# Column updates of a bisection on VectorE: one instruction on all columns, or one per column with a scalar operand

## The chip, the cores and the metric

The kernel runs on one core of a Trainium2 chip. Its engines are TensorE (PE in the profile, its weight loads PEld), VectorE (DVE), ScalarE (ACT), GpSimd (POOL) and SyncE (SP), which issues the DMAs here. Each engine takes its instructions in program order and waits for semaphores where an operand comes from elsewhere, or from an earlier instruction of its own that is still under way. The metric is the time of one execution on the device in microseconds (us), the median of the runs.

## What is computed

One decoder layer for 1024 tokens of width 1024, in float32. The part that matters here picks, for each query token, the 256 keys with the highest indexer score; softmax attention then runs over those keys alone:

```python
logits = jnp.einsum('bqhd,bsd->bqhs', iqb, ik_f) * (IDX_DIM ** -0.5)
score = jnp.einsum('bqh,bqhs->bqs', w, jax.nn.relu(logits))
score = jnp.where(causal[None], score, -jnp.inf)
_, idx = lax.top_k(score, k_sel)            # k_sel = 256
s = jnp.einsum('bqhd,bqkhd->bhqk', qb, kg) * (HEAD_DIM ** -0.5)
p = jax.nn.softmax(jnp.where(valid, s, -jnp.inf))
```

Around it stand one combined projection (q, k, v, indexer, pooling channels), a causal multi-scale pooling of 512 channels, an output projection, two layer norms with conditioning, and a gated feed-forward network.

## The kernel before, in words

The tokens lie in eight tiles of 128 rows; tile i has 128(i + 1) possible keys. Tiles 0 and 1 need no selection. For each of the others the kernel finds the 256th highest score of every row by bisection on the bits of the score, without sorting: `bisect` (line 643) first turns the scores into 16-bit keys, searches the upper half in 15 rounds, then the lower half in 16. A round counts for each row how many keys reach a candidate threshold (the buffer `cand`), and moves the candidate by half the last step, up or down.

Two engines search at once. ScalarE takes tiles 5 and 4 together and tile 3 (`search_a`, buffers colsA). VectorE takes tile 2 alone (buffers colsE, "the E search") and tiles 7 and 6 together (buffers colsD, "the D search"), in `search_v` (line 675). Such a buffer holds a few numbers per row of a tile; a number for each of nt tiles is nt neighbouring columns. A round of `search_v` has one counting pass per tile (lines 681 and 682: a tensor_scalar over up to 1024 keys whose accumulator gives the count; in the profile TENSOR_SCALAR_CACHE_REDUCE and DVE_READ_ACCUMULATOR) and then two small instructions on all nt columns at once: line 683 writes `pr`, the step where the count is high enough and zero otherwise, and line 685 adds it, with a constant, to `cand`. The next round's passes need that `cand`.

The search runs beside other work: the last indexer scores, the projections q, u, k and v on TensorE, the pooling and the rotary embedding on GpSimd. Places in VectorE's queue that others wait for are `u_split` (line 863: a pass over the pooling channels, written to ub_V, which ScalarE rounds to phi_V and GpSimd splits to plo_V for TensorE's matmuls "po"), and the two subtractions in `k_transpose` (kr_K, after TensorE's transposes kT and ScalarE's copies). GpSimd also splits the weights (ws_W) that TensorE multiplies with next. The attention (`u_exp`) begins with tile 7 and needs its finished selection.

The order on VectorE, ScalarE and GpSimd is fixed while the kernel is built. Every search is a Python generator that yields an engine and an estimated time before each piece. A `Queue` for each engine adds up its estimated time (`cost`, line 138; at least 0.16 us for any VectorE instruction), and `fill` (line 768) puts a search piece in wherever it is estimated to end before the next ordinary instruction could begin, give or take a slack. So more instructions in a round also move where later rounds stand. TensorE, and in the attention the other engines as well, are ordered by a scheduler.

Almost all instructions are issued by one helper line (169), so the profile's rows are told apart by the names of their buffers.

Of the kernel before, what the change touches and what calls it, by code (L numbers as in the profile page):

```python
# [18 lines left out]
ALU = mybir.AluOpType  # L19
# [162 lines left out]
def decoder_layer_kernel(  # L182
# [8 lines left out]
    V, A, G, T, SP = (Queue(tc, e, n, pinned, times) for e, n in  # L191
                      ((nc.vector, "V"), (nc.scalar, "A"), (nc.gpsimd, "G"), (nc.tensor, "T"), (nc.sync, "S")))
# [450 lines left out]
    def bisect(tiles, cols, on_act):  # L643

        nt = len(tiles)
        col = lambda q: cols[:, q * 4 : q * 4 + nt]
        cntc, kp, sg, cand, pr, M, ng, th, ib, thr = (col(q) for q in range(10))
# [3 lines left out]
        def trash(i):  # L651
            return ((junkA if 5 in tiles else junkB) if on_act else junkd(i))[:, 0 : P * (i + 1)]

        one = lambda c, m: c[:, m : m + 1]
# [20 lines left out]
        def search_v(bits, base, low):  # L675
            V.memset(cand, float(1 << (bits - 1)))
            for b in range(bits - 1, -1, -1):
                yield "V", 0.4 + 1.08 * sum_w + 0.35 * nt
                for m, i in enumerate(tiles):
                    dt = U16 if low else I16  # L680
                    V.tensor_scalar(trash(i).bitcast(dt), kv[i].bitcast(dt), one(cand, m), one(base, m),
                                    ALU.is_ge, ALU.add, accum_out=one(cntc, m))
                V.tensor_scalar(pr, cntc, 0.0, float(1 << b), ALU.is_ge, ALU.mult)
                off = -float(1 << (b - 1)) if b > 0 else -1.0
                V.scalar_tensor_tensor(cand, pr, off, cand, ALU.add, ALU.add)

        def search_a(bits, low):

# [13 lines left out]
            V.tensor_scalar(cand, cand, -1.0, None, ALU.mult)  # L702

        yield from (search_a(15, False) if on_act else search_v(15, kp, False))
        V.tensor_copy(M, cand)
        for m, i in enumerate(tiles):
# [5 lines left out]
            if on_act:  # L712
                V.tensor_scalar(one(thr, m), one(ng, m), 2.0, float(P * (i + 1) + 1), ALU.mult, ALU.add)
        yield from (search_a(16, True) if on_act else search_v(16, ng, True))

        V.tensor_copy(ib.bitcast(I32), M)
# [421 lines left out]
    for n_, u in enumerate(units):  # L1138
        g, pr, i = u
# [767 lines left out]
```

## Time and profile before

| what | value |
|---|---|
| time, median of 3 runs | 1324.58 us (1322.65 to 1326.92) |
| profiled execution: span | 1321.4 us |
| median of the runs less that span | 3.2 us |
| TensorE busy | 1199.6 us (91%) |
| VectorE busy | 1066.3 us (81%), 1828 instructions |
| GpSimd busy | 736.7 us (56%) |
| ScalarE busy | 648.6 us (49%) |

For the profiled execution the profile gives the span, from its first to its last instruction, and no other time of its own.

The page cuts the span into 40 slices of 33 us; a digit is the busy share in tenths:

```profile
PE   8979895797988996999789999999999999999996
...
DVE  6899999999978797477697787776878777777698
ACT  3346673675998776445534243333333333333531
POOL 1392373666213355427678384664848475576848
```

The searches on VectorE lie in slices 4 to 12 (about 117 to 374 us). VectorE is at 9 or more in nearly all of them, and TensorE dips to 5 and 7 in slices 7 and 8. The attention follows, to about 570 us, and then the output projection and the feed-forward part, where TensorE is busy almost throughout.

The rows of a timeline read: start in us, duration in us, engine, line, operation, output<-input, shapes and count; a bracket at the end gives how long the engine was idle before the row, and the instruction that ended the wait. A row with a count above one merges several.

### The profile page before, as it was taken

Reading aid. Unit: us, or ns where it says so; the run is one execution under the profiler, and the core shown is the slowest. Engines: PE = TensorE matmul, PEld = TensorE weight load, DVE = VectorE, ACT = ScalarE, POOL = GpSimd, SP = SyncE. Lnnn points to the kernel's source line nnn. Section 1 sums busy time; section 2 is a strip of 40 time slices with the busy share of each in tenths; the row PEclk is TensorE's granted clock in tenths of the full one; section 3 lists DMA queues with packets and bytes.
Section 4 is the critical chain, followed back from the end, with each engine's and each line's share of the span. In section 5 each row is a group of like instructions: output and inputs, shape, how many; then the busy total and the mean of one; then the engine's idle time right before and its main releaser. Section 6 shows DMA issues by size and latency. Waiting matters only on the chain.

```text
span 1321.4 us, 16106 instructions
## 1 busy us (share of the span) xinstructions
PE 1199.6 (91%) x5462; PEld 934.3 (71%) x5462; DVE 1066.3 (81%) x1828; ACT 648.6 (49%) x1335; POOL 736.7 (56%) x509
## 2 busy tenths in 40 slices
PE   8979895797988996999789999999999999999996
PEld 6646564575855654787677787878788887878775
DVE  6899999999978797477697787776878777777698
ACT  3346673675998776445534243333333333333531
POOL 1392373666213355427678384664848475576848
PEclk8999898798979998999799999999999999999998
DMA  9540020131100266420020101102010111113112
GB/s 343 222 158 29 16 72 24 64 96 42 47 16 9 73 215 239 144 72 9 32 96 32 65 32 64 64 32 96 33 64 32 65 43 53 68 44 112 47 58 119
DMA packets 34904, 103.91 MB, mean 79 GB/s; under 512 B 3843, under 2 KB 3843, under 8 KB 33286
## 3 DMA queue, kind: packets, MB, share of 16 engines
q1 hardware_dynamic: 34822, 102.88, 22.1%
q8 instruction: 43, 0.70, 0.2%
q14 instruction: 39, 0.32, 0.1%
HBM read 93.42 MB, written 9.45 MB: 78 GB/s over the span
## 4 chain that ended last, share of the span: by engine, by line
PE 38%; DVE 6%; POOL 4%; issue 2%; ACT 1%; DVEq 0%; POOLq 0%; ACTq 0%
PE gu L169 24%; PE dn L169 14%; DVE act_W L169 2%; POOL wraw_R L169 1%; DVE utmp_X L169 1%; POOL wraw_W L169 1%; DVE gtmp_V L169 1%; POOL wblk_T L169 0%; DVE wblk_T L169 0%; DVE hr_H L169 0%; POOL hr_H L169 0%; DVE res_X L169 0%; DVE stat_C L169 0%; POOL wblk_V L169 0%; DVE wblk_V L169 0%
## 5 line engine op out<-in xcount | busy, mean ns | idle before, releaser
L169 PE MATMUL gu<-hr_H,wblk_T 128*128 128x512 f32 (+1 forms) x924 | 217.3, 387 | 3.0 <-POOL wblk_T L169 1.9
L169 PE MATMUL gu<-hr_H,wblk_V 128*128 128x512 f32 (+1 forms) x924 | 215.2, 384 | 3.7 <-POOL wblk_V L169 1.9
L169 PEld LDWEIGHTS gu<-hr_H,wblk_T 128*128 128x128 f32 x924 | 172.3, 191 | 39.2 <-POOL wblk_T L169 3.6
L169 PEld LDWEIGHTS gu<-hr_H,wblk_V 128*128 128x128 f32 x924 | 170.0, 188 | 40.1 <-POOL wblk_V L169 3.6
L169 DVE TENSOR_TENSOR res_X<-res_X,dn 128x512 f32<-128x512 f32 (+1 forms) x253 | 159.0, 678 | 15.4 <-PE dn L169 15.3
L169 POOL TENSOR_SCALAR sm_H<-sm_H,stat_X 128x1024 f32<-128x1024 f32 (+7 forms) x64 | 58.6, 928 | 124.1 <-DVE stat_X L169 112.5
L169 PE MATMUL pj<-ws_W,hT_H 128*128 128x512 f32 x456 | 119.4, 409 | 4.4 <-ACT pout_K L169 2.0
L169 POOL TENSOR_TENSOR wraw_R<-wraw_R 128x512 f32<-128x512 f32 x64 | 94.5, 1484 | 46.9 <-DVE wblk_T L169 23.7
L169 POOL TENSOR_TENSOR wraw_W<-wraw_W 128x512 f32<-128x512 f32 x60 | 86.7, 1452 | 58.0 <-DVE wblk_V L169 29.3
L169 PEld LDWEIGHTS pj<-ws_W,hT_H 128*128 128x128 f32 x456 | 85.1, 192 | 30.0 <-issue 10.1
L169 PE MATMUL dn<-wblk_T,act_W 128*128 128x512 f32 x324 | 79.6, 394 | 4.4 <-DVE act_W L169 4.4
L169 PE MATMUL dn<-wblk_V,act_W 128*128 128x512 f32 x324 | 78.5, 391 | 2.9 <-DVE act_W L169 2.5
L169 DVE TENSOR_SCALAR_CACHE_REDUCE junk_X<-keysD_T,colsD_X 128x1024 int16<-128x1024 int16 (+1 forms) x64 | 78.9, 1269 | 0.7
L169 ACT ACTIVATE wblk_V<-wraw_R 128x512 fp32r<-128x512 f32 x56 | 35.2, 629 | 80.7 <-POOL wraw_R L169 62.3
L169 PEld LDWEIGHTS dn<-wblk_T,act_W 128*128 128x128 f32 x324 | 60.9, 189 | 19.1 <-DVE act_W L169 6.5
L169 PEld LDWEIGHTS dn<-wblk_V,act_W 128*128 128x128 f32 x324 | 60.4, 188 | 17.4 <-DVE act_W L169 4.2
L169 POOL TENSOR_TENSOR ws_W<-raw_R,ws_W 128x1024 fp32r<-128x1024 f32 x17 | 44.8, 2652 | 48.6 <-ACT ws_W L169 48.5
L169 ACT ACTIVATE wblk_V<-wraw_W 128x512 fp32r<-128x512 f32 x53 | 33.1, 627 | 75.0 <-POOL wraw_W L169 56.4
L169 ACT ACTIVATE wblk_T<-wraw_W 128x512 fp32r<-128x512 f32 x56 | 35.0, 628 | 66.3 <-POOL wraw_W L169 50.2
L169 ACT ACTIVATE wblk_T<-wraw_R 128x512 fp32r<-128x512 f32 x52 | 32.5, 627 | 60.9 <-POOL wraw_R L169 45.5
L169 ACT ACTIVATE junkA_T<-keys_T,colsA_X 128x768 bf16<-128x768 uint16 (+3 forms) x62 | 54.1, 873 | 9.0 <-DVE colsA_X L169 8.7
L169 ACT ACTIVATE utmp_X<-gu 128x512 f32<-128x512 f32 x33 | 19.7, 598 | 73.4 <-PE gu L169 73.4
(300 smaller groups left out, 2828.1 us busy)
## 6 DMA issues: line engine op xcount, KB each, us to landing
wm_K<-in_wma_dram SPq DMA_DIRECT2D x16, 512.0 KB, 9.5
modraw_V<-in_wmc_dram SPq DMA_DIRECT2D x16, 512.0 KB, 4.5
wraw_R<-in_wg_dram SPq DMA_DIRECT2D x6, 1024.0 KB, 4.9
wraw_R<-in_wd_dram SPq DMA_DIRECT2D x12, 512.0 KB, 3.5
wraw_W<-in_wup_dram SPq DMA_DIRECT2D x12, 512.0 KB, 3.5
modraw_V<-in_wmg_dram SPq DMA_DIRECT2D x10, 512.0 KB, 4.3
wraw_R<-in_wup_dram SPq DMA_DIRECT2D x10, 512.0 KB, 3.5
wraw_W<-in_wg_dram SPq DMA_DIRECT2D x5, 1024.0 KB, 4.9
```

Of the source, the lines that this page charges most:

```text
L169: ins_ = f(*a, **k)
```

## The change

```diff
@@ -680,9 +680,11 @@
                     V.tensor_scalar(trash(i).bitcast(dt), kv[i].bitcast(dt), one(cand, m), one(base, m),
                                     ALU.is_ge, ALU.add, accum_out=one(cntc, m))
-                V.tensor_scalar(pr, cntc, 0.0, float(1 << b), ALU.is_ge, ALU.mult)
                 off = -float(1 << (b - 1)) if b > 0 else -1.0
-                V.scalar_tensor_tensor(cand, pr, off, cand, ALU.add, ALU.add)
+                for m in range(nt):
+                    V.tensor_scalar(one(pr, m), one(cntc, m), 0.0, float(1 << b), ALU.is_ge, ALU.mult)
+                for m in range(nt):
+                    V.tensor_scalar(one(cand, m), one(pr, m), one(cand, m), off, ALU.add, ALU.add)
```

`one(c, m)` is column m of c. The update of `cand` was a scalar_tensor_tensor with two tensor inputs, `pr` and `cand`; now it is a tensor_scalar whose input is one column of `pr`, whose first scalar operand is the old candidate column and whose second is the constant. The value computed is the same. In the D search (nt = 2) a round now has four small instructions instead of two, in the E search (nt = 1) two as before; there are 31 rounds in each. The estimate that the generator yields for a round is as it was, but the `Queue` counts each instruction as it is issued, so a D round comes to 0.32 us more in it.

The places of the searches' pieces move with that. In the rows below, junk<-keysD is a counting pass of the D search, junk<-keysA with colsE one of the E search, and the rows on colsD or colsE alone are the small instructions. VectorE, the last rounds ahead of the second u_split, before:

```order
L169 TENSOR_SCALAR junk_X_614,colsE_X_616<-keysA_X_605,colsE_X_616 128x384
L169 TENSOR_SCALAR junk_X_607,colsD_X_615<-keysD_T_609,colsD_X_615 128x1024
L169 TENSOR_SCALAR junk_X_608,colsD_X_615<-keysD_T_609,colsD_X_615 128x896
L169 TENSOR_SCALAR colsE_X_616<-colsE_X_616 128x1
L169 TENSOR_SCALAR colsD_X_615<-colsD_X_615 128x2
L169 SCALAR_TENSOR_TENSOR colsE_X_616<-colsE_X_616 128x1
L169 SCALAR_TENSOR_TENSOR colsD_X_615<-colsD_X_615 128x2
L169 CAST colsE_X_616<-colsE_X_616 128x1
```

The same place now, from the last D round on:

```order
L169 TENSOR_SCALAR junk_X_607,colsD_X_615<-keysD_T_609,colsD_X_615 128x1024
L169 TENSOR_SCALAR junk_X_608,colsD_X_615<-keysD_T_609,colsD_X_615 128x896
L169 TENSOR_SCALAR colsD_X_615<-colsD_X_615 128x1
L169 TENSOR_SCALAR junk_X_614,colsE_X_616<-keysA_X_605,colsE_X_616 128x384
L169 TENSOR_SCALAR colsD_X_615<-colsD_X_615 128x1 x3
L169 TENSOR_SCALAR colsE_X_616<-colsE_X_616 128x1 x2
L169 TENSOR_SCALAR junk_X_614,colsE_X_616<-keysA_X_605,colsE_X_616 128x384
L169 TENSOR_SCALAR colsE_X_616<-colsE_X_616 128x1 x2
```

Behind these, four more E rounds of the last two rows follow before the CAST that ends the E search. Before, E's passes stood inside D's rounds there; now five of them stand alone. Ahead of the first u_split 26 E passes are issued instead of 30, and 12 D passes as before.

The second place is VectorE between the D search and the subtractions kr_K, at the end of the upper half of ScalarE's search. Before, these rows stood behind 42 D passes, and another D round came before the row on keys_T:

```order
L169 TENSOR_SCALAR colsA_X_606<-colsA_X_606 128x1
L169 TENSOR_TENSOR kr_K_1238<-kT_1902,kr_K_1238 64x4x128 x2
L169 TENSOR_SCALAR junk_X_607,colsD_X_615<-keysD_T_609,colsD_X_615 128x1024
L169 TENSOR_SCALAR junk_X_608,colsD_X_615<-keysD_T_609,colsD_X_615 128x896
L169 TENSOR_SCALAR colsD_X_615<-colsD_X_615 128x2
L169 SCALAR_TENSOR_TENSOR colsD_X_615<-colsD_X_615 128x2
L169 TENSOR_SCALAR junkA_T_612,colsA_X_606<-keys_T_611,colsA_X_606 128x768
```

Now, behind 40 D passes:

```order
L169 TENSOR_SCALAR junkA_T_612,colsA_X_606<-keys_T_611,colsA_X_606 128x768
L169 CAST colsA_X_606<-colsA_X_606 128x2
L169 SCALAR_TENSOR_TENSOR keys_T_611<-keys_T_611,colsA_X_606,score_X_77 128x768
L169 TENSOR_SCALAR colsA_X_606<-colsA_X_606 128x1
L169 TENSOR_SCALAR colsA_X_606<-colsA_X_606 128x2
```

The first kr_K now stands behind the row on keys_T, and every later kr_K has one D round fewer ahead of it, so one more stands behind the last: four instead of three. GpSimd's and SyncE's order is unchanged up to buffer numbers.

## The prediction

> **What bounds the kernel now.** I read the table of windows first, for the stretch in which the search runs. Its columns are the window, its length, then the busy time (and instructions) of TensorE, its weight loads, VectorE, ScalarE and GpSimd, the granted TensorE clock, the DMA share and GB/s.
>
> ```profile
> span 1321.4 us, 16106 instructions
> ...
> 244.00:283.00 39.00, 29.98 (x117) 23.02 (x116) 38.27 (x49) 27.75 (x68) 25.09 (x14) 0.87 0.31 95
> 283.00:330.00 47.00, 35.62 (x145) 28.25 (x144) 45.49 (x82) 26.83 (x61) 33.36 (x22) 0.89 0.16 51
> 330.00:372.00 42.00, 42.00 (x191) 34.04 (x190) 39.09 (x76) 40.41 (x121) 6.96 (x6) 1.00 0.11 38
> ```
>
> From 244 to 330 us VectorE is busy 83.8 of 86 us and TensorE 65.6: VectorE sets the pace. From 330 to 372 TensorE is busy throughout, at full clock, and ScalarE 40.4 of 42. So time taken from VectorE counts fully only until TensorE becomes the later one. Next come the groups of the search's small instructions (count, busy us, mean ns), and the minimum/median/maximum of the same from the view by tile. colsD is the search of tiles 7 and 6 ("D"), colsE that of tile 2 ("E").
>
> ```profile
> L169 DVE SCALAR_TENSOR_TENSOR colsD_X<-colsD_X 128x2 f32<-128x2 f32 x31 | 18.4, 592 | 0.7
> L169 DVE TENSOR_SCALAR colsD_X<-colsD_X 128x2 f32<-128x2 f32 x33 | 18.0, 546 | 0.8
> L169 DVE SCALAR_TENSOR_TENSOR colsE_X<-colsE_X 128x1 f32<-128x1 f32 x31 | 11.5, 371 | 0.6
> ...
> L169 DVE TENSOR_SCALAR colsD_X<-colsD_X x39: 130/170/2162, 181.0 to 367.4; 128x2 f32<-128x2 f32 x33, 128x1 f32<-128x1 f32 x4, 128x2 int16<-128x2 f32 x1, 128x2 int32<-128x2 int32 x1
> L169 DVE SCALAR_TENSOR_TENSOR colsD_X<-colsD_X x31: 156/161/2282, 194.9 to 360.3; 128x2 f32<-128x2 f32 x31
> L169 DVE TENSOR_SCALAR colsE_X<-colsE_X x37: 136/148/154, 117.9 to 241.6; 128x1 f32<-128x1 f32 x35, 128x1 int16<-128x1 f32 x1, 128x1 int32<-128x1 int32 x1
> L169 DVE SCALAR_TENSOR_TENSOR colsE_X<-colsE_X x31: 145/160/1265, 125.7 to 239.9; 128x1 f32<-128x1 f32 x31
> ```
>
> An instruction on two numbers per partition takes 0.16 us at the median and up to 2.28. Only the one-column tensor_scalar never does that: 37 of them, none over 154 ns. The timeline shows where the long ones come from.
>
> ```profile
> 319.67 9.51 POOL L169 TENSOR_TENSOR ws_W<-raw_R,ws_W 128x1024 fp32r<-128x1024 f32 x4
> ...
> 319.88 2.16 DVE L169 TENSOR_SCALAR colsD_X<-colsD_X 128x2 f32<-128x2 f32 x1
> 322.08 2.28 DVE L169 SCALAR_TENSOR_TENSOR colsD_X<-colsD_X 128x2 f32<-128x2 f32 x1
> ```
>
> GpSimd's four instructions take 2.38 us each. The two-column tensor_scalar ends at 322.04, when the first of them does, and the scalar_tensor_tensor at 324.36, with the second. They wait for GpSimd, one of its instructions each.
>
> **The change part by part.** *Removed waits.* The excess over the medians is 18.4 - 31 x 0.161 = 13.4, 18.0 - 33 x 0.170 = 12.4 and 11.5 - 31 x 0.160 = 6.5 us. Two of the 33 stand ahead of the loop and stay; I give them 1.7 us. That leaves 30.6 us, 24.1 of it in the D search. Where D's lie, the same groups in 244 to 283 and then in 283 to 372 tell:
>
> ```profile
> L169 DVE SCALAR_TENSOR_TENSOR colsD_X<-colsD_X 128x2 f32<-128x2 f32 x6 | 6.8, 1141 | 0.2
> L169 DVE TENSOR_SCALAR colsD_X<-colsD_X 128x2 f32<-128x2 f32 x6 | 6.4, 1062 | 0.2
> ...
> L169 DVE SCALAR_TENSOR_TENSOR colsD_X<-colsD_X 128x2 f32<-128x2 f32 x16 | 7.7, 484 | 0.5
> L169 DVE TENSOR_SCALAR colsD_X<-colsD_X 128x2 f32<-128x2 f32 x16 | 6.3, 394 | 0.6
> ```
>
> Less 0.165 each, that is 11.2 us in the first window, 8.7 in the second, and so 4.2 before 244.
>
> Does the new form wait? Its first half (one column, two constants) is the E row above. Its second half has a column as scalar operand; the nearest rows are those of layer norm, one-column tensor_scalars of which most read columns as scalars.
>
> ```profile
> L169 DVE TENSOR_SCALAR stat_C<-stat_C x174: 134/214/275, 569.8 to 1315.6; 128x1 f32<-128x1 f32 x142, 128x1 int32<-128x1 int32 x32
> ...
> 586.73 2.45 DVE L169 TENSOR_SCALAR stat_C<-stat_C 128x1 f32<-128x1 f32 x11
> ...
> 586.86 1.28 POOL L169 TENSOR_TENSOR stage_W<-stage_W 128x512 f32<-128x512 f32 x1
> ...
> 119.11 0.27 DVE L169 TENSOR_SCALAR colsA_X<-colsA_X 128x1 f32<-128x1 f32 x3
> ```
>
> Eleven of them ran through a GpSimd instruction in 2.45 us, and of all 174 none took over 275 ns. So I take no wait, and 0.214 us for the new second half.
>
> *Added instructions.* D rounds have four small instructions for two. Three independent ones took 0.27 us together (last row), so such instructions start some 0.06 us apart. A quiet round, D alone; then rounds of D with E in between, and E alone:
>
> ```profile
> 287.68 1.34 DVE L169 TENSOR_SCALAR_CACHE_REDUCE junk_X<-keysD_T,colsD_X 128x1024 uint16<-128x1024 uint16 x1
> ...
> 290.08 0.08 DVE L169 DVE_READ_ACCUMULATOR junk_X<-keysD_T,colsD_X 128x1 f32 x1
> ...
> 290.43 0.16 DVE L169 SCALAR_TENSOR_TENSOR colsD_X<-colsD_X 128x2 f32<-128x2 f32 x1
> 290.63 1.34 DVE L169 TENSOR_SCALAR_CACHE_REDUCE junk_X<-keysD_T,colsD_X 128x1024 uint16<-128x1024 uint16 x1
> ...
> 211.49 1.33 DVE L169 TENSOR_SCALAR_CACHE_REDUCE junk_X<-keysD_T,colsD_X 128x1024 int16<-128x1024 int16 x1
> ...
> 214.87 1.33 DVE L169 TENSOR_SCALAR_CACHE_REDUCE junk_X<-keysD_T,colsD_X 128x1024 int16<-128x1024 int16 x1
> ...
> 222.13 0.67 DVE L169 TENSOR_SCALAR_CACHE_REDUCE junk_X<-keysA_X,colsE_X 128x384 uint16<-128x384 uint16 x1
> ...
> 223.23 0.67 DVE L169 TENSOR_SCALAR_CACHE_REDUCE junk_X<-keysA_X,colsE_X 128x384 uint16<-128x384 uint16 x1
> ```
>
> A D round takes 2.95 us, 0.55 of it from the last accumulator read to the next count. In the new round tile 7's first instruction need not wait for tile 6's count, tile 6's fills the gap, and the next count waits for tile 7's pair alone: 0.148 + 0.214 + two gaps of 0.035 us (290.43 + 0.16 to 290.63) = 0.43. Were the four to run in series, it would be 2 x 0.148 + 2 x 0.214 + 4 x 0.035 + 0.11 (before the first) = 0.97. So a round changes by -0.12 to +0.42 us; I take -0.12, since the row of three shows overlap. An E round has no second tile to fill it: 1.10 becomes 1.155.
>
> By the Trainium skill, "VectorE: DVE Perf Modes", section "Rules for kernel authors", chained instructions pay a pipeline flush each, and one should minimise their count. That speaks against this edit; it stands for the series, rival 2. The row of three disagrees with it.
>
> *Moved work.* The planner counts 0.16 us for each small instruction, so D rounds look 0.32 us longer to it and E rounds fall behind: four E rounds move from before the first u_split to after it, and five then run alone ahead of the second. A round alone costs 1.155 us, one inside a D round 214.87 - 211.49 - 2.95 = 0.43. Five times 0.7 is 3.5 us later at the second u_split.
>
> *What reaches the end.* I follow the chain by the waits in brackets.
>
> ```profile
> 226.03 1.22 DVE L169 SCALAR_TENSOR_TENSOR ub_V<-ub_V,ub_V 128x1024 f32<-128x1024 f32 x1
> ...
> 244.24 1.22 DVE L169 SCALAR_TENSOR_TENSOR ub_V<-ub_V,ub_V 128x1024 f32<-128x1024 f32 x1
> ...
> 228.88 1.22 PE L169 MATMUL po<-phi_V,wps_X 128*128 128x512 f32 x2 [15.09 <-ACT ub_V L169]
> ...
> 255.48 7.71 PE L169 MATMUL pair<-ws_W,hT_H 128*128 128x512 f32 x24 [4.30 <-POOL ws_W L169]
> 264.84 5.55 PE L169 MATMUL pair<-ws_W,hT_H 128*128 128x512 f32 x23 [1.65 <-POOL ws_W L169]
> ...
> 287.20 5.73 PE L169 MATMUL pj<-ws_W,hT_H 128*128 128x512 f32 x24 [1.96 <-ACT pout_K L169]
> ...
> 304.15 1.09 PE L169 MATMUL kT<-const_C,rope_V 128*128 128x128 f32 x4 [4.84 <-DVE kr_K L169]
> ...
> 322.07 8.29 PE L169 MATMUL pair<-ws_W,hT_H 128*128 128x512 f32 x23 [4.33 <-POOL ws_W L169]
> ...
> 349.76 1.39 DVE L169 TENSOR_TENSOR kr_K<-kT,kr_K 64x512 fp32r<-64x512 f32 x2 [1.86 <-ACT kr_K L169]
> ...
> 373.17 0.63 DVE L169 TENSOR_SCALAR score_X<-junk_X 128x896 f32<-128x896 bf16 x1
> ```
>
> 1. First u_split (226.03): E's 6.5 us of waits, the share of D's 4.2 that its first two rounds ahead of 205 us had (I take 0.7) and the four moved E rounds (about 2.2) go, the slower E round costs 26 x 0.055 = 1.4: 8.0 us earlier. TensorE waited 15.1 us here, so it follows.
> 2. Second u_split (244.24): the other 3.5 of D's 4.2 us go; the moved rounds come back (2.2), running alone costs 3.5, the rest of E 0.3. 8.0 + 3.5 - 6.0 = 5.5 us earlier.
> 3. From 244 to 283 VectorE loses its largest waits, 11.2 us, but both brackets there name GpSimd's split of weights (ws_W), and GpSimd starts from the second u_split, with the same work ahead of the split as before. The third u_split is no longer the late one, so the 1.65 us wait shrinks to about 0.5, no more: 1.1. VectorE gets ahead here, and later has to wait for TensorE.
> 4. TensorE's wait for pout (ScalarE reaches it earlier) falls by about 1.6; the one for kr_K goes, since VectorE has gained more than that by then (5.5 us in step 2 and most of 11.2 in step 3): 4.8; that for the V weights, which hangs on ScalarE's and GpSimd's rotary work, falls by about 2. With shorter idle the 23 matmuls of 8.29 us should come nearer to the 5.73 of 24: 2, an estimate from these two rows.
> 5. TensorE's unbroken stretch from 330 on thus starts 5.5 + 1.1 + 1.6 + 4.8 + 2 + 2 = 17 us earlier. The last kr_K (349.76) waits for TensorE's transposes by way of ScalarE, so it comes at 332.8. Behind it stood 373.8 - 351.15 = 22.65 us of VectorE work with three D rounds; now there are four: 22.65 + 2.83 - 3 x 0.12 = 25.1. The selection ends at 334.2 + 25.1 = 359.3 instead of 373.8: **14.5 us** earlier.
>
> The attention behind it starts from that selection; its work is the same, in a slightly different order. The span becomes 1321.4 - 14.5 = 1306.9; 3.2 us lie between the span and the median of the runs (1324.58). Predicted: **1310 us**.
>
> **The rivals.** *1: nearly all arrives.* If GpSimd's chain of step 3 shortens as well (its instructions may hold waits for VectorE of their own) and TensorE keeps full clock, VectorE's 30.6 - 3.5 + 1.2 = 28 us come through: 1324.6 - 28 = 1296. Against it stands TensorE's full window. 12%.
>
> *2: the four run in series.* 0.54 us per round more than I took, on nine D rounds before the second u_split and four at the end: 7 us, so 1317. For it: each of the four reads what another wrote shortly before. 9%.
>
> *3, the other side: the column operand waits for GpSimd too.* The place is 244 to 283, where both small instructions of a round waited 1.1 us on the mean; with four that wait, each for another GpSimd instruction, D's 24.1 us double. By the share that reaches the end (14.5 of 30.6) that is 11 us: 1336. It decides as soon as one-column rows exceed 1 us. Against it is the layer norm row. 3%.
>
> *4: given back behind 372.* ScalarE, 40.4 of 42 us busy up to there, also runs the search of tiles 5, 4 and 3; if it does not move up with the rest, or the altered order in the attention costs as much, the time stays at about 1323. Its work before 330 moves up though (26.8 of 47 us busy). 8%.
>
> **How the numbers follow.** The forecast has 68%, with 1304 to 1316 as its own range (steps 3 and 4 by 4 us either way, and the round's price). The range goes from rival 1 to beyond rival 2, 1296 to 1318; rivals 3 and 4 and the edges are left out. A measurement tells 0.3% apart, 4 us. Faster by more: forecast, rival 1 and most of rival 2, 87%; within: rival 4 and the rest, 8%; slower 5%.
>
> **What would show it.** One-column rows at 0.15 and 0.21 us with maxima below 0.3 us (step 1); D rounds of 2.8 us; u_split at 218 and 239 us; TensorE without its wait for kr_K; a VectorE that now waits for kT between 290 and 335; the selection done at 359. Maxima over 1 us would make the first term wrong, D rounds of 3.4 us the second, and a selection at 346 step 3.

## The result, and the profile after

The change takes **1308.55 us** (median of 4 runs, 1307.95 to 1309.86), against 1323.90 us for the kernel before in the same comparison: ratio **0.9886**, 95% interval 0.9864 to 0.9908. Predicted were 1310 us and a range of 1296 to 1318. The profiled execution has a span of 1306.2 us (1321.4 before, 1306.9 predicted). One of the six executions of a kernel further down, the one with GpSimd's instructions halved, took 4011.72 us and is left out of its ratio.

The windows of the change first (columns as before). From 244 to 330 us VectorE is busy 75.1 of 86 us instead of 83.8, TensorE 78.0 instead of 65.6.

```profile
span 1306.2 us, 16165 instructions
...
244.00:283.00 39.00, 35.08 (x140) 27.88 (x140) 36.68 (x85) 31.10 (x81) 32.71 (x20) 0.86 0.39 122
283.00:330.00 47.00, 42.94 (x198) 35.21 (x197) 38.40 (x98) 37.83 (x94) 28.72 (x19) 0.96 0.11 34
```

The groups of small instructions (busy us, mean ns), then the E search's view by tile, with minimum/median/maximum:

```profile
L169 DVE TENSOR_SCALAR colsD_X<-colsD_X 128x1 f32<-128x1 f32 x128 | 16.8, 178 | 0.0
L169 DVE TENSOR_SCALAR colsE_X<-colsE_X 128x1 f32<-128x1 f32 x66 | 11.7, 178 | 1.3
...
L169 DVE TENSOR_SCALAR colsD_X<-colsD_X 128x2 f32<-128x2 f32 x2 | 2.5, 1234 | 0.0
...
L169 DVE TENSOR_SCALAR colsE_X<-colsE_X x68: 134/154/215, 116.6 to 235.7; 128x1 f32<-128x1 f32 x66, 128x1 int16<-128x1 f32 x1, 128x1 int32<-128x1 int32 x1
```

The one-column instructions have a mean of 0.178 us, about midway between the 0.148 and 0.214 of the prediction. In the two searches only the two rows of two columns that are left, in the set-up ahead of the loop, still wait. But new waits stand at instructions that the change doesn't touch, the set-up of ScalarE's search of tiles 5 and 4. Its two-column rows (colsA, on VectorE) from the timeline, before and then after:

```profile
153.07 0.16 DVE L169 TENSOR_SCALAR colsA_X<-colsA_X 128x2 f32<-128x2 f32 x1
...
153.26 0.35 DVE L169 TENSOR_SCALAR colsA_X<-colsA_X 128x2 f32<-128x2 f32 x4
...
149.81 1.26 DVE L169 TENSOR_SCALAR colsA_X<-colsA_X 128x2 f32<-128x2 f32 x1
...
151.11 1.47 DVE L169 TENSOR_SCALAR colsA_X<-colsA_X 128x2 f32<-128x2 f32 x4
```

They took 0.51 us together and take 2.73 now: 2.2 us are lost again here, ahead of the first u_split. The first of them now falls under a GpSimd instruction and ends with it (GpSimd's runs from 149.29 to 151.05); before, both rows were over when GpSimd began its next one (154.63). What a D round looks like now, and what GpSimd does meanwhile, from the timeline:

```profile
253.30 1.33 DVE L169 TENSOR_SCALAR_CACHE_REDUCE junk_X<-keysD_T,colsD_X 128x1024 int16<-128x1024 int16 x1
...
255.69 0.52 DVE L169 TENSOR_SCALAR colsD_X<-colsD_X 128x1 f32<-128x1 f32 x4
256.12 1.34 DVE L169 TENSOR_SCALAR_CACHE_REDUCE junk_X<-keysD_T,colsD_X 128x1024 int16<-128x1024 int16 x1
...
228.37 0.67 DVE L169 TENSOR_SCALAR_CACHE_REDUCE junk_X<-keysA_X,colsE_X 128x384 uint16<-128x384 uint16 x1
...
229.53 0.67 DVE L169 TENSOR_SCALAR_CACHE_REDUCE junk_X<-keysA_X,colsE_X 128x384 uint16<-128x384 uint16 x1
...
255.12 2.39 POOL L169 TENSOR_TENSOR ws_W<-raw_R,ws_W 128x1024 fp32r<-128x1024 f32 x1
```

The four take 0.52 us together in the middle of a GpSimd instruction of 2.39 us, and the round 2.82 us (253.30 to 256.12). A lone E round takes 1.16 (228.37 to 229.53). The rows that answer to the chain of the prediction: VectorE's four u_splits, TensorE's waits, then kr_K and the last row of the selection.

```profile
217.74 1.22 DVE L169 SCALAR_TENSOR_TENSOR ub_V<-ub_V,ub_V 128x1024 f32<-128x1024 f32 x1
...
238.31 1.22 DVE L169 SCALAR_TENSOR_TENSOR ub_V<-ub_V,ub_V 128x1024 f32<-128x1024 f32 x1
...
247.21 3.35 DVE L169 SCALAR_TENSOR_TENSOR ub_V<-ub_V,ub_V 128x1024 f32<-128x1024 f32 x1 [2.04 <-POOL ub_V L169]
...
262.39 1.23 DVE L169 SCALAR_TENSOR_TENSOR ub_V<-ub_V,ub_V 128x1024 f32<-128x1024 f32 x1
...
220.59 1.22 PE L169 MATMUL po<-phi_V,wps_X 128*128 128x512 f32 x2 [9.86 <-ACT ub_V L169]
...
249.53 13.56 PE L169 MATMUL pair<-ws_W,hT_H 128*128 128x512 f32 x47 [3.92 <-POOL ws_W L169]
...
305.21 7.09 PE L169 MATMUL pair<-ws_W,hT_H 128*128 128x512 f32 x23 [4.06 <-POOL ws_W L169]
...
314.01 1.39 DVE L169 TENSOR_TENSOR kr_K<-kT,kr_K 64x512 fp32r<-64x512 f32 x2 [3.03 <-ACT kr_K L169]
...
331.60 1.39 DVE L169 TENSOR_TENSOR kr_K<-kT,kr_K 64x512 fp32r<-64x512 f32 x2 [1.87 <-ACT kr_K L169]
...
357.96 0.63 DVE L169 TENSOR_SCALAR score_X<-junk_X 128x896 f32<-128x896 bf16 x1
```

From 249.53 to the V weights (305.21) TensorE has no bracket left where it had four (1.65, 1.96, 4.84 and, at 310.96, 0.26 us): the waits for pout_K and kr_K are gone. VectorE is the one that waits for kT now (3.03 us at 314). The selection ends 15.2 us earlier, and so does the span.

### The profile page after: what moved, and what is told of

It reads as the page before. It is cut to its first block, busy times and chain, and to the rows that moved or that the text cites. A ratio compares the mean times of both kernels' runs of the same rounds, so it can differ in the third digit from the quotient of the medians.

```text
span 1306.2 us, 16165 instructions
## 1 busy us (share of the span) xinstructions
PE 1193.9 (91%) x5462; PEld 930.6 (71%) x5462; DVE 1043.9 (80%) x1890; ACT 649.0 (50%) x1335; POOL 734.9 (56%) x509
## 4 chain that ended last, share of the span: by engine, by line
PE 38%; DVE 7%; POOL 4%; issue 2%; ACT 1%; DVEq 0%; POOLq 0%; ACTq 0%
PE gu L169 24%; PE dn L169 14%; DVE act_W L169 2%; POOL wraw_R L169 1%; DVE utmp_X L169 1%; POOL wraw_W L169 1%; DVE gtmp_V L169 1%; POOL wblk_T L169 1%; DVE wblk_T L169 0%; DVE hr_H L169 0%; POOL hr_H L169 0%; DVE res_X L169 0%; DVE stat_C L169 0%; POOL wblk_V L169 0%; DVE wblk_V L169 0%
## 5 line engine op out<-in xcount | busy, mean ns | idle before, releaser
L169 ACT ACTIVATE sm_H<-sm_H,stat_X 128x1024 f32<-128x1024 f32 (+7 forms) x64 | 49.1, 768 | 15.2 <-DVE stat_X L169 15.0
```

The lines of the kernel that those rows point to most:

```text
L169: ins_ = f(*a, **k)
```

## The experiments

All times were measured beside the kernel before; spans and starts are of one profiled execution each. The last three columns give starts in us, from the timelines of VectorE: the first kr_K, the last one, and the last row of D's selection.

| kernel | median us | ratio, 95% interval | span | first kr_K | last kr_K | selection |
|---|---|---|---|---|---|---|
| before | 1321.8 to 1323.9 | 1 | 1321.4 | 302.6 | 349.8 | 373.2 |
| the change | 1308.6 | 0.9886 (0.9864 to 0.9908) | 1306.2 | 285.5 | 331.6 | 358.0 |
| the change, again | 1308.6 | 0.9894 (0.9872 to 0.9916) | 1307.4 | 287.0 | 333.1 | 359.5 |
| old instructions, new count | 1324.2 | 1.0029 (1.0016 to 1.0041) | 1322.4 | 302.0 | 348.2 | 374.6 |
| new instructions, old count | 1305.6 | 0.9879 (0.9860 to 0.9899) | 1303.6 | 287.0 | 333.5 | 356.9 |
| D only | 1309.5 | 0.9913 (0.9897 to 0.9929) | 1306.8 | 287.7 | 333.8 | 360.2 |
| E only | 1323.1 | 1.0011 (1.0002 to 1.0020) | 1322.6 | 300.1 | 347.3 | 373.8 |
| pr only | 1321.8 | 1.0007 (0.9992 to 1.0021) | 1320.0 | 299.4 | 346.4 | 372.8 |
| cand only | 1318.6 | 0.9978 (0.9966 to 0.9991) | 1317.2 | 295.6 | 342.6 | 369.4 |
| cand, pr on 3 columns | 1318.9 | 0.9984 (0.9971 to 0.9998) | 1317.4 | 296.5 | 342.8 | 369.5 |
| before, GpSimd halved | 1314.6 | 0.9939 (0.9917 to 0.9961) | 1313.1 | 296.8 | 341.1 | 364.5 |
| pairs | 1308.0 | 0.9896 (0.9871 to 0.9921) | 1305.3 | 285.1 | 331.4 | 358.0 |
| set-up in columns too | 1302.7 | 0.9855 (0.9834 to 0.9876) | 1298.8 | 281.5 | 327.8 | 351.2 |
| the same, GpSimd halved | 1300.9 | 0.9836 (0.9811 to 0.9861) | 1298.7 | 282.3 | 326.0 | 349.4 |

The table holds the main reading. From the last row of the selection to the end of the span it is 946.7 to 949.3 us in every kernel. From the first kr_K to the last it is 46.1 to 47.3 us, except where GpSimd's instructions are halved (about 44). From the last kr_K to the selection it is 23.4 us with three D rounds behind it and 26.4 to 26.8 with four. What a kernel gains is what it gains ahead of the **first kr_K**, and by the number of D rounds left at the end.

Single starts and spans are to be read with one caution. From 102 to 112 us the granted TensorE clock was 1.00 in the profiled executions of the change, old instructions in the new count, E only, pairs and set-up in columns; it was 0.83 in the others, and 0.66 in the two with GpSimd halved. The two executions of the change, at 1.00 and 0.83, are 1.5 us apart from the first u_split to the selection.

### Old instructions, new count; new instructions, old count

In the first kernel the planner counts the two old instructions of a D round like four; in the second it counts the four new ones like two.

```diff
+                V.small = float(nt)        # first kernel; second: 1.0 / nt
                 V.tensor_scalar(pr, cntc, 0.0, float(1 << b), ALU.is_ge, ALU.mult)
...
+                V.small = 1.0
```
```diff
-        return max(0.16, ...)
+        return self.small * max(0.16, ...)
```

> The two multi-column instructions of before, standing in the order of the change (the planner counts a D round as long as the changed one). Theory A, the gain comes from the waits for GpSimd that the new instructions don't have: no gain here, and the moved work costs by itself, five E rounds alone ahead of the second u_split (3.5 us) and one more D round at the end (2.9 us), so about 1328 us (1324 to 1333), with colsD rows above 2 us. Theory B, the altered order brings the gain (the first u_split is no longer queued behind four E rounds): about 1309 us.

> The one-column instructions of the change in the order of before (the planner counts them at half in the D search). Theory A: the moved work was a cost that the change pays, so without it the second u_split comes about 3 us earlier than with the change (235 instead of 238.3 us), three D rounds instead of four stand behind the last kr_K (2.8 us), and the time is about 1303 us (1299 to 1306). Theory B: without the new order most of the gain is lost, about 1320 us. If TensorE's chain and not the order sets the end, it stays at 1308.

Theory B falls: old instructions in the new count are 0.29% slower than before, new ones in the old count 1.21% faster. The instructions bring the gain. But the moved work isn't what I had said, and so the two came out 4 us below and 3 above what I expected. VectorE's program from the first D round on (D and E are counting rounds, u a u_split, k a kr_K pair; one D and one E in all is the single count between the halves of a search):

```
before                       DEEEEEDEDEDEDEEEEE u DEDED u DD u DDDD u DDDDDDkDkkkDkDDkDDDkDkDDD
the change                   DEEEEEDDDEDDEEEEE u DDDEEEEEE u DD u DDDD u DDDDDkDkkkDkDDkDDDkDkDDDD
old instructions, new count  DEEEEEDEDEDEDEEEEE u DEDED u DD u DDDD u DDDDDkDkkkDkDDkDDDkDkDDDD
new instructions, old count  DEEEEEDDDEDDEEEEE u DDDEEEEEE u DD u DDDD u DDDDDDkDkkkDkDDkDDDkDkDDD
```

The planner's count moves one D round only, from ahead of the first kr_K to the very end. The place of the E rounds follows the instructions, whatever the planner counts. So these two kernels don't undo the lone E rounds, and the 235 us that I expected for the second u_split could not come: it starts at 239.78. The change run again and the new instructions in the old count, timeline rows of the last kr_K and the last row of the selection:

```profile
333.13 1.39 DVE L169 TENSOR_TENSOR kr_K<-kT,kr_K 64x512 fp32r<-64x512 f32 x2 [1.87 <-ACT kr_K L169]
...
359.49 0.63 DVE L169 TENSOR_SCALAR score_X<-junk_X 128x896 f32<-128x896 bf16 x1
...
333.50 1.39 DVE L169 TENSOR_TENSOR kr_K<-kT,kr_K 64x512 fp32r<-64x512 f32 x2 [1.98 <-ACT kr_K L169]
...
356.90 0.63 DVE L169 TENSOR_SCALAR score_X<-junk_X 128x896 f32<-128x896 bf16 x1
```

26.4 us with the fourth round, 23.4 without: the round costs 3.0 us at the end. Ahead of the first kr_K it is free, since VectorE has time there (it starts at 287.0 in both). The spans differ by 2.6 and 3.8 us from those of the change; the times by 0.07 and 0.15%, less than their intervals.

### D only, E only

In the second of these two the planner counts the old instructions of a D round like four.

```diff
+                if nt == 2:      # E only: nt == 1
                     (the two loops of the change)
+                else:
                     (the two instructions of before)
```

> The new form only in the search of tiles 7 and 6, the old one in that of tile 2; order as with the change. Theory A: E's 6.5 us of waits stay, all before the first two u_splits; the second u_split comes some 5 us later than with the change, TensorE follows, and the time is about 1313 us (1311 to 1316). Rival: VectorE's later waits for kT take it up, and the time stays at 1309.

> The new form only in the search of tile 2, the old one in that of tiles 7 and 6; order as with the change. Theory A: D's 24 us of waits stay; of the change's gain what E's part brings ahead of the second u_split is left (some 5 us), less the moved work (3.5 and 2.9 us), so about 1324 us (1319 to 1327). Together with the D-only kernel the two gains should add up to that of both over the old instructions in the new order. Rival: E's part alone, which lies ahead of everything, carries most of the gain, about 1313 us.

Against the old instructions in the same count (1.0029) D alone brings 1.16%, E alone 0.18%, both 1.35 to 1.43%: they add up within the intervals. E is worth less than I said. The D-only kernel's first u_split starts at 221.31, 2.1 us behind the second run of the change (219.2), and its second at 240.47, 0.7 us behind (239.8) and not 5: one lone E round fewer stands between the two. The traces show what takes up a part of it: the set-up rows of colsA. In the D-only kernel they still take 0.16 and 0.17 us; where E's instructions are new, in the change and in the E-only kernel, two of them take 1.25 to 1.28 us each. So 2.2 us of what E's new form saves are lost on colsA. In the E-only kernel D's rise as well: ahead of the first u_split its two-column instructions take 9.1 us, 4.8 with the old instructions in the same count.

### One of the two instructions alone

In both kernels the planner counts a D round as it counts the changed one.

```diff
 # pr only
-                V.tensor_scalar(pr, cntc, 0.0, float(1 << b), ALU.is_ge, ALU.mult)
+                for m in range(nt):
+                    V.tensor_scalar(one(pr, m), one(cntc, m), 0.0, float(1 << b), ALU.is_ge, ALU.mult)
                 V.scalar_tensor_tensor(cand, pr, off, cand, ALU.add, ALU.add)
 # cand only
                 V.tensor_scalar(pr, cntc, 0.0, float(1 << b), ALU.is_ge, ALU.mult)
-                V.scalar_tensor_tensor(cand, pr, off, cand, ALU.add, ALU.add)
+                for m in range(nt):
+                    V.tensor_scalar(one(cand, m), one(pr, m), one(cand, m), off, ALU.add, ALU.add)
```

> Only the first small instruction (pr) goes to one column each; the scalar_tensor_tensor on all columns stays. ScalarE's and GpSimd's order as with the change. Theory A (each waiting instruction costs its own wait for GpSimd): of the 30.6 us of waits D's 10.7 in pr go, 19.9 in the scalar_tensor_tensors stay; D's part in the new order brought about 15 us for 24.1 us of waits, so this brings 15 x 10.7 / 24.1 = 6.7 us over the 1324 us of the old instructions in the new order: about 1317 us (1314 to 1320). Rival: the scalar_tensor_tensor inherits the wait (it is held by the same GpSimd instruction and only waits longer), then about 1323 us and a scalar_tensor_tensor mean above 0.7 us.

> Only the second small instruction (cand) goes to one column each, as a tensor_scalar with the old candidate as scalar operand; the tensor_scalar on all columns (pr) stays. Order of ScalarE and GpSimd as with the change. Theory A: D's 13.4 and E's 6.5 us of waits go, D's 10.7 in pr stay: 15 x 13.4 / 24.1 = 8.5 and E's 2 to 3 us, about 1313 us (1310 to 1316). Rival: the waits move to pr, about 1321 us with pr's mean above 0.7 us in the D search.

Both brought much less than was expected. Against the old instructions in the same count (1.0029), pr alone brings 0.22% and cand alone 0.51%, some 3 and 7 us, where both together bring 1.35 to 1.43%, 18 to 19 us. (By the spans it is 2.4, 5.2 and 15 to 16 us; the early clock blurs these.) Did the other instruction inherit the waits? The groups of the old instructions in the new count (two rows), of pr only, and of cand only:

```profile
L169 DVE SCALAR_TENSOR_TENSOR colsD_X<-colsD_X 128x2 f32<-128x2 f32 x31 | 20.6, 664 | 0.7
...
L169 DVE TENSOR_SCALAR colsD_X<-colsD_X 128x2 f32<-128x2 f32 x33 | 16.7, 507 | 0.8
...
L169 DVE SCALAR_TENSOR_TENSOR colsD_X<-colsD_X 128x2 f32<-128x2 f32 x31 | 17.9, 577 | 0.7
...
L169 DVE TENSOR_SCALAR colsD_X<-colsD_X 128x2 f32<-128x2 f32 x33 | 21.8, 660 | 0.7
```

In the pr-only kernel it didn't (577 ns for 664); in the cand-only kernel it did, by 5.1 us (21.8 for 16.7). The rest was lost later, as TensorE's waits show, pr only first:

```profile
300.96 1.09 PE L169 MATMUL kT<-const_C,rope_V 128*128 128x128 f32 x4 [4.71 <-DVE kr_K L169]
...
297.12 1.09 PE L169 MATMUL kT<-const_C,rope_V 128*128 128x128 f32 x4 [3.55 <-DVE kr_K L169]
```

The wait for kr_K, 4.84 us before, stands in both. It is 3.55 to 4.92 us in every kernel in which one or both of D's instructions work on several columns, and gone in every kernel in which neither does, D only among them. And in both kernels here the third u_split already takes 3.35 us instead of 1.21. So the waits don't have a fixed worth, and "15 us for 24.1, so 6.7 for 10.7" was a wrong sum.

### Three columns

The edit, against the cand-only kernel; the third column is zeroed ahead of the loop:

```diff
+            V.memset(cols[:, 2:3], 0.0)
...
-                V.tensor_scalar(pr, cntc, 0.0, float(1 << b), ALU.is_ge, ALU.mult)
+                if nt == 2:      # the D search
+                    V.tensor_scalar(cols[:, 16:19], cols[:, 0:3], 0.0, float(1 << b), ALU.is_ge, ALU.mult)
```

> As the cand-only kernel, but the D search's pr runs on three columns instead of two (the third column holds a zero and is not used). Which property of the two-column tensor_scalar makes it wait? Theory 1, that it works on more than one number per row: 128x3 rows wait as the 128x2 rows do, up to 2 us, and the time is that of the cand-only kernel, about 1313 us. Theory 2, that the number is even (two elements can be handled as a pair, three can't): no 128x3 row above 0.3 us, and the time is that of the whole change, about 1308 us.

```profile
L169 DVE TENSOR_SCALAR colsD_X<-colsD_X 128x3 f32<-128x3 f32 x31 | 19.7, 636 | 0.7
```

Theory 1: three numbers per row wait like two (0.64 us on the mean), and the time is that of cand only (0.9984 and 0.9978), though not the 1313 us expected for both. What goes free is a tensor_scalar on one number per row. One number alone isn't enough: the scalar_tensor_tensor of E, on one column too but with two tensor inputs, waited up to 1.265 us before.

### GpSimd's instructions halved, VectorE's unchanged

The split of the weights is shown; the pooling's sums and its split (plo_V) are cut in the same way.

```diff
-        (lo_eng or V).tensor_tensor(dst[:, n : 2 * n], raw, f_(dst[:, 0:n]), ALU.subtract)
+        for h in range(2 if lo_eng is G else 1):   # each half of the columns
+            (lo_eng or V).tensor_tensor(...)
```

> The kernel before with its multi-column instructions unchanged; instead GpSimd's 1024-column tensor_tensors (the weight splits, the pooling's shifted sums and the split of phi) are cut into two of 512 columns. GpSimd's work and nearly all of the order are the same. Theory A, a small VectorE instruction waits for the one GpSimd instruction that runs: no colsD or colsE row above about 1.3 us (2.3 before), D's waits between the second and the fourth u_split fall from 11.2 to about 6 us, and the time falls by some 2 to 5 us to about 1318. Rival, the long rows come from VectorE itself or from a semaphore that only coincides with GpSimd: rows of 2.2 us stay, and the time stays at 1322 or rises by the extra GpSimd instructions.

The view by tile of this kernel (maxima 2162 and 2282 ns before):

```profile
L169 DVE TENSOR_SCALAR colsD_X<-colsD_X x39: 131/171/1308, 181.5 to 358.8; 128x2 f32<-128x2 f32 x33, 128x1 f32<-128x1 f32 x4, 128x2 int16<-128x2 f32 x1, 128x2 int32<-128x2 int32 x1
L169 DVE SCALAR_TENSOR_TENSOR colsD_X<-colsD_X x31: 149/162/1210, 193.3 to 351.7; 128x2 f32<-128x2 f32 x31
```

With no instruction of VectorE altered, and one E round moved behind the first u_split, the longest rows fall to what half a GpSimd instruction takes (four of its ws_W instructions of 512 columns take 5.01 us at 258.96, 1.25 each). That shows that the long rows are waits for GpSimd. The time fell by 0.61%, 8 us, more than expected. Not all of that is waits, which fall from 11.2 to 6.9 us in D between the second and the fourth u_split. TensorE also gets the V weights in halves, and its 4.33 us for them become two short brackets:

```profile
315.20 0.98 PE L169 MATMUL pair<-ws_W,hT_H 128*128 128x512 f32 x3 [1.84 <-POOL ws_W L169]
316.45 4.85 PE L169 MATMUL pair<-ws_W,hT_H 128*128 128x512 f32 x20 [0.27 <-POOL ws_W L169]
```

### The order of the four

```diff
                 for m in range(nt):
                     V.tensor_scalar(one(pr, m), ...)
-                for m in range(nt):
                     V.tensor_scalar(one(cand, m), ...)
```

> The change with its four small instructions of a D round in another order: pr and cand of tile 7, then pr and cand of tile 6, so that each cand stands right behind the pr that it reads. Overlap theory: an instruction waits only for the one it reads, and tile 6's pr slips in behind tile 7's cand: a quiet D round of 2.85 to 2.95 us (2.83 with the change), the time within 2 us of the change. Series theory (each dependent instruction pays in full, the rival 2 of the prediction): 3.2 to 3.4 us a round, and 1311 to 1314 us.

```profile
249.95 1.33 DVE L169 TENSOR_SCALAR_CACHE_REDUCE junk_X<-keysD_T,colsD_X 128x1024 int16<-128x1024 int16 x1
...
252.34 0.70 DVE L169 TENSOR_SCALAR colsD_X<-colsD_X 128x1 f32<-128x1 f32 x4
252.96 1.33 DVE L169 TENSOR_SCALAR_CACHE_REDUCE junk_X<-keysD_T,colsD_X 128x1024 int16<-128x1024 int16 x1
```

A round of 3.01 us lies between the two expectations: each cand behind its own pr costs 0.18 us a round. It costs no time that these runs resolve (0.9896 against 0.9894).

### A faster version

> The change with the planner's count of a D round as before, and in addition the three two-column instructions that set a search up (pr, sg, flip: in the profile of the change rows of 1.26, 1.47 and 2.48 us on colsA and colsD, of which about 4.5 us are waits) written per column. Theory A: these waits go as well, all ahead of the first u_split, where TensorE waits 9.9 us: both u_splits come 4 us earlier than with the planner's old count alone (215 and 236 us), and the time is 2 to 4 us below its 1305.6 us: about 1302 us. Rival: GpSimd's or ScalarE's order takes it up, 1305.5 us.

> The fastest version so far (one-column rounds and set-up, the planner's old count of a D round) with the same halved GpSimd instructions. Theory A: the third u_split, a scalar_tensor_tensor that takes 3.35 us there for 1.22 elsewhere, waits for half a GpSimd instruction less (about 2.3 us), and the other large passes gain as little; the extra GpSimd instructions cost some tenths of a us on the chain ahead of the weights: 1302 us, within 2 us of the version without. Rival: VectorE's instructions now hold GpSimd up twice as often, and the time rises by 3 us or more.

```diff
-        V.tensor_scalar(pr, cntc, float(TOPK), None, ALU.is_ge)
-        V.tensor_scalar(sg, pr, 2.0, -1.0, ALU.mult, ALU.add)
+        for m in range(nt):
+            V.tensor_scalar(one(pr, m), one(cntc, m), float(TOPK), None, ALU.is_ge)
+        for m in range(nt):
+            V.tensor_scalar(one(sg, m), one(pr, m), 2.0, -1.0, ALU.mult, ALU.add)
...
```

With the set-up in columns and the planner's old count the u_splits start at 212.86 and 234.14, and the time is 1302.7 us, 1.45% below before. Its span is 7 to 9 us shorter than the change's, and their two intervals overlap by little (0.9834 to 0.9876, and 0.9864 to 0.9908). All of colsD's 135 tensor_scalars, as the view by tile of this kernel has them:

```profile
L169 DVE TENSOR_SCALAR colsD_X<-colsD_X x135: 129/154/213, 176.6 to 345.5; 128x1 f32<-128x1 f32 x132, 128x1 int16<-128x1 f32 x2, 128x2 int32<-128x2 int32 x1
```

Halved GpSimd instructions on top give 1300.9 us, which its interval doesn't separate from that, but which lies wholly below the change's.

> The change itself once more, on the same chip as the others, for a direct comparison: ratio to before 0.9886, about 1307 us; between the version with the planner's old count (1305.6) and the D-only kernel (1309.5).

The same ratio within the intervals, but the profile of this run differs early on. TensorE's rows at 105 us, the first run's, the second's, and those of the kernel before:

```profile
105.21 2.11 PE L169 MATMUL pj<-ws_W,hT_H 128*128 128x512 f32 x8
...
105.40 3.46 PE L169 MATMUL pj<-ws_W,hT_H 128*128 128x512 f32 x8
...
105.30 3.10 PE L169 MATMUL pj<-ws_W,hT_H 128*128 128x512 f32 x8
```

The same eight matmuls take 2.11 or 3.46 us in two executions of one kernel, with a granted clock of 1.00 and 0.60 from 105 to 109 us (0.64 before). The two are 1.5 us apart at the first u_split (217.74 and 219.24).

## Why the prediction was right, step by step

**Removed waits: right, and shown, but 2.2 us are lost again elsewhere.** Halving GpSimd's instructions halved the longest rows, and the one-column tensor_scalars don't wait at all. What the prediction left out is that other multi-column instructions, moved to another time, may meet GpSimd at work, as colsA's set-up rows now do. The Trainium skill, "SBUF — State Buffer", section "Who interferes with whom", has VectorE's second port pair shared with GpSimd: an instruction of VectorE in a two-port mode contends for it, as does one with two SBUF inputs if GpSimd reads SBUF, and whichever comes first has it for its whole instruction. The rows of 1.2 to 1.3 us for halves and 2.2 to 2.3 us for wholes agree.

**The price of the new form: right.** D rounds take 2.82 us (2.83 predicted), lone E rounds 1.16 (1.155). Rival 2, the series, would have needed 3.4; even with the order turned against it the round takes 3.01. Rival 3 fell with the maximum of 215 ns (E's rows; D's one-column rows in the set-up-in-columns kernel 213).

**Moved work: size right, cause wrong.** I put the lone E rounds down to the planner's 0.16 us for each instruction. They stay when the planner counts as before, so it is not the planner that places them. What places them was not isolated; that the new instructions fill the gaps of D rounds in which E rounds stood is a guess. From the first u_split to the second it is 20.57 us, 18.21 before; the prediction's terms give 20.7. The extra D round at the end does come from the planner, and costs 3.0 us.

**Step 1: 8.0 us predicted, 8.3 measured, partly by luck.** 1.4 us of the 8.3 stem from the clock at 105 us (VectorE's wait for ScalarE's relu_K at 112 us, behind those matmuls, is 0.68 us; it was 1.96 before). Like against like, the second run has 6.8. The sum was 1.2 us too high. The 2.2 us that are lost on colsA are not in it, and are more than that; smaller differences in other rows go both ways. **Step 2** follows: 5.5 predicted, 5.9 and 4.4 measured.

**Step 3: right for TensorE, and something missed on VectorE.** TensorE's second pair of projections ends at 263.09 (249.53 + 13.56) instead of 270.39. That is 7.3 us, 5.95 of them had by its first pair: 1.35 for the 1.1 predicted. VectorE needs 24.1 us from the second u_split to the fourth instead of 31.3, though 11.2 us of waits are gone. The third u_split gives 4.2 back: 2.04 idle for GpSimd's ub_V, and 3.35 us for an instruction of 1.21. It has two tensor inputs, and it starts at 247.21, just behind a split of weights on GpSimd:

```profile
247.13 5.67 POOL L169 TENSOR_TENSOR ws_W<-raw_R,ws_W 128x1024 fp32r<-128x1024 f32 x2
```

GpSimd is held in turn: these two splits take 5.67 us, 0.9 more than two at 2.39 each.

**Step 4: the sum right, one term wrong.** pout_K: 1.96 gone (1.6 predicted). kr_K: 5.1 with the small one (4.8). The 23 matmuls: 8.29 to 7.09, 1.2 for 2. The V weights: I let that wait fall by 2, and it fell from 4.33 to 4.06; what it hangs on moved up with TensorE, not ahead of it. What made up for it lies between the two: from the end of the second pair to the V weights it is 42.12 us instead of 51.68. That is 9.6, of which waits are 7.3; the remaining 2.2 us fit the granted clock, 0.96 from 283 to 330 where it was 0.89. 1.2 of them are in one row, the 19 matmuls behind the wait for kr_K: 5.81 us before (at 304.89), 4.58 now (at 289.96).

**Step 5: right.** The last kr_K starts at 331.6 (332.8 predicted), four D rounds follow, and the selection ends at 358.6 (359.3). That is 15.2 us earlier, in the second run 13.7, and the 14.5 predicted lie between. Behind the selection nothing is gained or lost (948.2 us from its last row to the end, before and after), so rival 4 fell; rival 1 fell because VectorE, once ahead, waits for TensorE.

**What the prediction could not say:** that the gain is not a share of the waits. It took 14.5 of 30.6 as such a share for rival 3, and my expectations for the single parts did the same. Counted as the groups' excess over their medians, the old instructions in the new count hold 33 us of waits in D and E. Pr alone takes away 10 of them and brings 3 us, cand alone 17 and 7, the change 31 and 18 to 19, for TensorE's wait for kr_K goes only when both of D's instructions work on one column each.

## What to carry to other kernels

Where VectorE and GpSimd work side by side, look at the maximum of a group of small instructions, not its median. Rows that end with a GpSimd instruction are likely waits for it; shorter GpSimd instructions test that. Here one-column tensor_scalars took most of the waits away, and some came back at other multi-column instructions that had moved. Price such a change at the one wait of the next engine that ends last, not by a share of the busy time: here either half of the change alone brought less than half of the gain. Where an order is planned by estimated costs, see that more and cheaper instructions don't change the count: here it put a round of 3 us at the end.

## What the hardware showed beyond that

Three columns per row wait for GpSimd as two do (0.636 us mean at 128x3, 0.660 at 128x2 in the cand-only kernel). A tensor_scalar on one column never does in these searches (maximum 0.217 us over all runs); a scalar_tensor_tensor on one column does (1.265 us before). The Trainium skill, "VectorE: DVE Perf Modes", section "Mode 2×_2P", lets a tensor_scalar use both ports where its outermost dimension above one is even, or equal in source and destination; three columns that wait agree with the second half of that. One-column instructions of 0.15 and 0.21 us, each pair dependent, run four in 0.52 us when two tiles alternate, and in 0.70 us when each follows the one it reads.
